# Rotary embedding on one core: the combines write bf16, and ScalarE widens the result to f32 before the store

## The chip, the cores and the metric

The kernel runs on one core of a Trainium2 chip. The metric is the device time of one execution in microseconds (us). The kernel before takes 165.52 us (median of 16 runs, 165.32 to 166.47). All runs named here are fast, with a granted clock of 1.0. The profiler's span is about 1.9 us shorter than the device time of the same run, so spans are compared with spans and times with times.

## The reference, cut to what matters

```python
# x: (16, 512, 1024) f32; cos, sin: (512, 32) f32; 16 heads of 64
x1, x2 = x[..., :32], x[..., 32:]          # per head
rotated = concatenate([x1 * cos - x2 * sin, x1 * sin + x2 * cos], axis=-1)   # f32
```

Each element is read once and written once: 33.55 MB in, 33.55 MB out, and 0.13 MB of tables. There is no matmul.

## The kernel before

One of the 16 batches is one tile: 128 partitions, four rows of 1024 f32 on each, 2 MB. SyncE's queue issues the loads, up to three tiles ahead. ScalarE (ACT) casts a tile to bf16 and issues the stores. VectorE (DVE) does four operations per tile: two multiplications (the products) and then a subtraction and an addition of their halves (here called the combines). The tables were widened once to 64 columns, each holding its 32 values twice.

```python
NX = 3    # buffers for loads       NC = 2   # casts
NO = 3    # results                 NTMP = 2 # products
# SyncE
for t in range(NT):
    if t >= NX: sp.wait_ge(sem_ci, t - NX + 1)          # cast t-3 done
    sp.dma_start(x_sb[:, xb, :], x_tile_ap(t)).then_inc(sem_in[xb], 16)
    # t == 0: also the two tables, 64 KB each
# ScalarE (the tables are cast first)
LEAD = 2
for it in range(NT + LEAD):
    t = it
    if t < NT:
        ae.wait_ge(sem_in[xb], 16 * (t // NX + 1))
        if t >= NC: ae.wait_ge(sem_vp, t - NC + 1)      # products t-2 done
        ae.activation(xb_sb[:, cb, :], x_sb[:, xb, :], ACT_COPY).then_inc(sem_ci, 1)
    u = it - LEAD
    if u >= 0:
        ae.wait_ge(sem_vf, u + 1)
        ae.dma_start(out_tile_ap(u), o_sb[:, ob, :]).then_inc(sem_out[ob], 16)
# VectorE (waits for buffers cut)
ve.tensor_tensor(t1v, xb_jhd(cb), coscat_b, mult)                           # L135
ve.tensor_tensor(t2v, xb_jhd(cb), sincat_b, mult).then_inc(sem_vp, 1)       # L136
ve.wait_ge(sem_vp, t + 1)
if t >= NO: ve.wait_ge(sem_out[ob], 16 * (t // NO))      # store t-3 landed
ve.tensor_tensor(orows[:, :, 0:HALF], t1[:, :, 0:HALF], t2[:, :, HALF:HD], subtract)       # L141
ve.tensor_tensor(orows[:, :, HALF:HD], t2[:, :, 0:HALF], t1[:, :, HALF:HD], add).then_inc(sem_vf, 1)  # L144
```

## Time and profile before

| | before |
|---|---|
| device time, median | 165.52 us |
| span of the profiled run | 164.6 us |
| VectorE busy | 142.5 us (87%) |
| ScalarE busy | 59.9 us (36%) |
| moved by DMA | 67.25 MB |

The page of the kernel before first gives the busy time of each engine; then the span in 40 slices, VectorE's busy tenths, DMA's busy tenths and the rate in GB/s.

```profile
DVE 142.5 (87%) x64; ACT 59.9 (36%) x21; POOL 0.2 (0%) x4
...
DVE  0007999999999999999999999999998989999930
...
DMA  5999999999999999999999999999999999999547
GB/s 171 434 418 422 442 438 366 422 430 434 438 430 418 446 426 438 418 438 430 442 422 426 442 430 430 422 436 434 434 422 430 438 438 426 418 446 382 255 191 318
```

Two rows of nines stand under each other: VectorE and DMA both look full. The groups of instructions of the kernel before: busy time in us and mean ns of one, then the idle time before them and what ended it.

```profile
L111 ACT ACTIVATE xb_sb<-x_sb 128x4096 bf16<-128x4096 f32 x16 | 57.8, 3615 | 74.2 <-DMA x_sb<-in_x_dram 37.6
L135 DVE TENSOR_TENSOR tmp_sb<-xb_sb,coscat_sb 128x4096 bf16<-128x4096 bf16 x16 | 36.6, 2285 | 13.2 <-ACT xb_sb L111 13.2
L141 DVE TENSOR_TENSOR o_sb<-tmp_sb 128x2048 f32<-128x2048 bf16 x16 | 36.7, 2292 | 2.2 <-DMA out_dram<-o_sb 1.6
L144 DVE TENSOR_TENSOR o_sb<-tmp_sb 128x2048 f32<-128x2048 bf16 x16 | 36.6, 2284 | 0.0
```

The combines have half the elements of the products and take the same time (2292 and 2284 ns for 2048 elements, 2285 ns for 4096). They differ in writing f32. The next view, the table of windows, shows whether DMA moves more where VectorE is not full. It gives length, busy time (and count) of VectorE, ScalarE and GpSimd, clock, DMA's busy share and GB/s of each stretch.

```profile
4.00:24.00 20.00, 10.78 (x5) 11.65 (x7) 0.00 (x0) 1.00 1.02 431
24.00:29.00 5.00, 4.96 (x4) 2.29 (x1) 0.00 (x0) 1.00 0.99 377
29.00:149.00 120.00, 117.89 (x54) 44.72 (x13) 0.00 (x0) 1.00 1.01 431
149.00:154.00 5.00, 4.97 (x3) 0.00 (x0) 0.00 (x0) 1.00 0.95 403
154.00:159.00 5.00, 3.86 (x2) 0.00 (x0) 0.00 (x0) 1.00 0.26 108
```

From 4 to 24 us VectorE is half idle, and DMA moves 431 GB/s. From 29 to 149 us VectorE is full, and DMA moves the same 431 GB/s. So 431 GB/s is what DMA gives in this kernel, whether VectorE is half idle or full. 67.25 MB at that rate is 156 us, to which the start comes (171 GB/s in the first of the 40 slices). That the rate is DMA's limit for these transfers rests on the two stretches here and on the run of the streams alone below, which has 432 GB/s from 29 to 149 us with no engine computing. After the start, the one large loss is at the end. Measured against 431 GB/s, the windows from 149 to 159 us lack (431-403)x5/431 + (431-108)x5/431 = 4.1 us of DMA's work. This missing work is called the hole below. The timeline of the kernel before says why (start, duration, engine, line):

```profile
155.58 2.29 DVE L144 TENSOR_TENSOR o_sb<-tmp_sb 128x2048 f32<-128x2048 bf16 x1
157.90 0.34 ACTq L116 DMA_DIRECT2D out_dram<-o_sb  x1
```

The loads end near 138 us. By the landing times in the trace, the stores of 4.5 tiles are left over then. The first 3.5 of them keep DMA busy until about 155 us, but VectorE releases the last one only at 157.9 us.

### The profile page before, as it was taken

What the parts mean: (1) busy time and instruction counts of PE and PEld (TensorE: products, weight loads), DVE (VectorE), ACT (ScalarE), POOL (GpSimd) and SP (SyncE); (2) the same over time, 40 slices, a digit from 0 to 9 for tenths busy, and PEclk for the clock granted to TensorE, in tenths of its full rate; (3) what the DMA queues carried; (4) which work ended last, traced back from release to release, by engine and by line L of the source; (5) the groups of instructions that cost most, each with busy time, mean ns of one, the idle gap of its engine ahead of it and who ended that gap; (6) DMA issues with size and microseconds to landing.
All of it is one profiled execution on the core that took longest, in us unless ns stands there. A gap on an engine that the chain in (4) does not pass through costs nothing.

```text
span 164.6 us, 190 instructions
## 1 busy us (share of the span) xinstructions
DVE 142.5 (87%) x64; ACT 59.9 (36%) x21; POOL 0.2 (0%) x4
## 2 busy tenths in 40 slices
DVE  0007999999999999999999999999998989999930
ACT  3088635335170808062433508052260804300000
POOL 0000000000000000000000000000000000000000
DMA  5999999999999999999999999999999999999547
GB/s 171 434 418 422 442 438 366 422 430 434 438 430 418 446 426 438 418 438 430 442 422 426 442 430 430 422 436 434 434 422 430 438 438 426 418 446 382 255 191 318
DMA packets 4897, 67.25 MB, mean 408 GB/s; under 512 B 544, under 2 KB 800, under 8 KB 800
## 3 DMA queue, kind: packets, MB, share of 16 engines
q1 hardware_dynamic: 2592, 33.69, 48.8%
q10 hardware_dynamic: 2304, 33.56, 47.7%
q14 instruction: 1, 0.01, 0.0%
HBM read 33.69 MB, written 33.55 MB: 408 GB/s over the span
## 4 chain that ended last, share of the span: by engine, by line
DMA 53%; DVE 25%; ACT 8%; issue 7%; DVEq 1%; SPq 0%; ACTq 0%
DMA x_sb<-in_x_dram 30%; DMA out_dram<-o_sb 19%; DVE tmp_sb L135 8%; DVE tmp_sb L136 8%; ACT xb_sb L111 8%; DVE o_sb L144 6%; DMA sin_sb<-in_sin_dram 4%; DVE o_sb L141 3%; DVEq L40 1%; SPq L88 0%; SPq L86 0%; ACT coscat_sb L96 0%; ACT sincat_sb L99 0%; ACT sincat_sb L98 0%; ACT coscat_sb L97 0%
## 5 line engine op out<-in xcount | busy, mean ns | idle before, releaser
L111 ACT ACTIVATE xb_sb<-x_sb 128x4096 bf16<-128x4096 f32 x16 | 57.8, 3615 | 74.2 <-DMA x_sb<-in_x_dram 37.6
L135 DVE TENSOR_TENSOR tmp_sb<-xb_sb,coscat_sb 128x4096 bf16<-128x4096 bf16 x16 | 36.6, 2285 | 13.2 <-ACT xb_sb L111 13.2
L141 DVE TENSOR_TENSOR o_sb<-tmp_sb 128x2048 f32<-128x2048 bf16 x16 | 36.7, 2292 | 2.2 <-DMA out_dram<-o_sb 1.6
L136 DVE TENSOR_TENSOR tmp_sb<-xb_sb,sincat_sb 128x4096 bf16<-128x4096 bf16 x16 | 36.6, 2285 | 0.0
L144 DVE TENSOR_TENSOR o_sb<-tmp_sb 128x2048 f32<-128x2048 bf16 x16 | 36.6, 2284 | 0.0
L96 ACT ACTIVATE coscat_sb<-cos_sb 128x128 bf16<-128x128 f32 x1 | 0.3, 309 | 6.6 <-DMA sin_sb<-in_sin_dram 6.6
L96 ACT ACT_TABLE_LOAD x1 | 1.3, 1283 | 0.7 <-PEq L162 0.7
L99 ACT ACTIVATE sincat_sb<-sin_sb 128x128 bf16<-128x128 f32 x1 | 0.3, 293 | 0.0
L97 ACT ACTIVATE coscat_sb<-cos_sb 128x128 bf16<-128x128 f32 x1 | 0.3, 292 | 0.0
L98 ACT ACTIVATE sincat_sb<-sin_sb 128x128 bf16<-128x128 f32 x1 | 0.3, 292 | 0.0
L162 POOL MEMSET const-bfloat16-1.0<- 128x1 bf16 x1 | 0.1, 102 | 0.0
L162 POOL MEMSET const-uint8-127<- 128x1 uint8 x1 | 0.1, 102 | 0.0
L162 POOL MEMSET const-float32-0.0<- 128x1 f32 x1 | 0.1, 99 | 0.2 <-issue 0.2
L162 POOL MEMSET const-float32-1.0<- 128x1 f32 x1 | 0.1, 99 | 0.0
## 6 DMA issues: line engine op xcount, KB each, us to landing
x_sb<-in_x_dram SPq DMA_DIRECT2D x16, 2048.0 KB, 21.2
out_dram<-o_sb ACTq DMA_DIRECT2D x16, 2048.0 KB, 17.8
cos_sb<-in_cos_dram SPq DMA_DIRECT2D x1, 64.0 KB, 7.3
sin_sb<-in_sin_dram SPq DMA_DIRECT2D x1, 64.0 KB, 7.0
```

Of the source, the lines that this page charges most:

```text
L40: with ExitStack() as stack:
L96: last = ae.activation(coscat_sb[:, :, 0:HALF], cos_sb[:, :, :], ACT_COPY)
L97: last = ae.activation(coscat_sb[:, :, HALF:HD], cos_sb[:, :, :], ACT_COPY)
L98: last = ae.activation(sincat_sb[:, :, 0:HALF], sin_sb[:, :, :], ACT_COPY)
L99: last = ae.activation(sincat_sb[:, :, HALF:HD], sin_sb[:, :, :], ACT_COPY)
L111: ae.activation(xb_sb[:, cb, :], x_sb[:, xb, :], ACT_COPY).then_inc(sem_ci, 1)
L135: ve.tensor_tensor(t1v, xb_jhd(cb), coscat_b, mult)
L136: ve.tensor_tensor(t2v, xb_jhd(cb), sincat_b, mult).then_inc(sem_vp, 1)
L141: ve.tensor_tensor(orows[:, :, 0:HALF], t1[:, :, 0:HALF], t2[:, :, HALF:HD], subtract)
L144: ve.tensor_tensor(orows[:, :, HALF:HD], t2[:, :, 0:HALF], t1[:, :, HALF:HD], add).then_inc(sem_vf, 1)
L162: nc = _bacc.Bacc("TRN2", target_bir_lowering=False, num_devices=1)
```

## The change

Its intent is to make VectorE's combines faster. They write a new bf16 tile `ob_sb`; ScalarE copies it to the f32 tile `o_sb` and issues the store. On ScalarE the copy out of tile t-2 now stands ahead of the cast of tile t. There are three cast buffers instead of two. A list of tiles is added that could split tiles, but all 16 stay whole. The core of the diff:

```diff
-    NC = 2
+    NC = 3
     NO = 3
+    NOB = 3
+        ob_sb = stack.enter_context(nc.sbuf_tensor([P, NOB, RE], bf16))
 ... (ScalarE's loop)
+                u = it - LEAD
+                if u >= 0:
+                    ae.wait_ge(sem_vf, u + 1)
+                    if u >= NO:
+                        ae.wait_ge(sem_out[ob], 16 * (u // NO))
+                    ae.activation(
+                        o_sb[:, ob, 0:Eu], ob_sb[:, obb, 0:Eu], ACT_COPY
+                    ).then_inc(sem_co, 1)
+                    ae.wait_ge(sem_co, u + 1)
+                    ae.dma_start(out_tile_ap(u), o_sb[:, ob, 0:Eu]).then_inc(sem_out[ob], 16)
                 t = it
                 if t < NT:
 ... (the cast, as before)
-                u = it - LEAD
-                if u >= 0:
-                    ae.wait_ge(sem_vf, u + 1)
-                    ae.dma_start(out_tile_ap(u), o_sb[:, ob, :]).then_inc(sem_out[ob], 16)
 ... (VectorE)
-                if t >= NO:
-                    ve.wait_ge(sem_out[ob], 16 * (t // NO))
+                if t >= NOB:
+                    ve.wait_ge(sem_co, t - NOB + 1)
+                obv = ob_sb[:, obb, 0:E].rearrange("p (r d) -> p r d", d=HD)
                 ve.tensor_tensor(
-                    orows[:, :, 0:HALF], t1[:, :, 0:HALF], t2[:, :, HALF:HD], subtract
+                    obv[:, :, 0:HALF], t1[:, :, 0:HALF], t2[:, :, HALF:HD], subtract
                 )
 ... (the addition likewise)
```

More of the change, by code (lines that the diff above doesn't have):

```diff
@@ L22, in bass_split_heads_rope_kernel, with _split @@
     SPP = seq // P
+    tiles = [(b, 0, SPP) for b in range(batch)]
+    def _split(tile, parts):
+        b, j0, nj = tile
+        if nj % parts != 0:
+            return [tile]
+        q = nj // parts
+        return [(b, j0 + i * q, q) for i in range(parts)]
+    if len(tiles) >= 2:
+        t_last = tiles.pop()
+        t_prev = tiles.pop()
+        tiles += [t_prev, t_last]
+    NT = len(tiles)
     ROWS = SPP * H
     RE = ROWS * HD
-    NT = batch
     NX = 3
-    NC = 2
+    NC = 3
     NO = 3
+    NOB = 3
     NTMP = 2
@@ L54, in bass_split_heads_rope_kernel @@
         sem_ci = stack.enter_context(nc.semaphore("sem_ci"))
+        sem_co = stack.enter_context(nc.semaphore("sem_co"))
         sem_vp = stack.enter_context(nc.semaphore("sem_vp"))
@@ L57, in bass_split_heads_rope_kernel @@
         block = stack.enter_context(nc.Block(no_gpsimd_drain=False))
-        cos_v = cos.rearrange("(p j) d -> p j d", p=P)
-        sin_v = sin.rearrange("(p j) d -> p j d", p=P)
+        cos_v = cos.rearrange("(p j) d -> p (j d)", p=P)
+        sin_v = sin.rearrange("(p j) d -> p (j d)", p=P)
         def x_tile_ap(t):
-            return x[t, :, :].rearrange("(p j) d -> p (j d)", p=P)
+            b, j0, nj = tiles[t]
+            v = x[b, :, :].rearrange("(p j) d -> p j d", p=P)
+            return v[:, j0:j0 + nj, :].rearrange("p j d -> p (j d)")
         def out_tile_ap(t):
-            return out[t, :, :, :].rearrange("(p j) h d -> p (j h d)", p=P)
-        def xb_jhd(cb):
-            return xb_sb[:, cb, :].rearrange("p (j h d) -> p j h d", j=SPP, h=H)
-        def o_rows(ob):
-            return o_sb[:, ob, :].rearrange("p (r d) -> p r d", d=HD)
-        coscat_b = coscat_sb[:, :, None, :].broadcast_to([P, SPP, H, HD])
-        sincat_b = sincat_sb[:, :, None, :].broadcast_to([P, SPP, H, HD])
+            b, j0, nj = tiles[t]
+            v = out[b, :, :, :].rearrange("(p j) h d -> p j (h d)", p=P)
+            return v[:, j0:j0 + nj, :].rearrange("p j e -> p (j e)")
         def uses(nbuf, b):
@@ L83, in _ @@
                 xb = t % NX
+                _, _, nj = tiles[t]
+                E = nj * H * HD
                 if t >= NX:
                     sp.wait_ge(sem_ci, t - NX + 1)
-                sp.dma_start(x_sb[:, xb, :], x_tile_ap(t)).then_inc(sem_in[xb], 16)
+                sp.dma_start(x_sb[:, xb, 0:E], x_tile_ap(t)).then_inc(sem_in[xb], 16)
                 if t == 0:
-                    sp.dma_start(cos_sb[:].rearrange("p j d -> p (j d)"),
-                                 cos_v.rearrange("p j d -> p (j d)")).then_inc(sem_tab, 16)
-                    sp.dma_start(sin_sb[:].rearrange("p j d -> p (j d)"),
-                                 sin_v.rearrange("p j d -> p (j d)")).then_inc(sem_tab, 16)
+                    sp.dma_start(
+                        cos_sb[:].rearrange("p j d -> p (j d)"), cos_v
+                    ).then_inc(sem_tab, 16)
+                    sp.dma_start(
+                        sin_sb[:].rearrange("p j d -> p (j d)"), sin_v
+                    ).then_inc(sem_tab, 16)
         @block.scalar
@@ L103, in _ @@
             for it in range(NT + LEAD):
+                u = it - LEAD
+                if u >= 0:
+                    ob = u % NO
+                    obb = u % NOB
+                    _, _, nju = tiles[u]
+                    Eu = nju * H * HD
+                    ae.wait_ge(sem_vf, u + 1)
[6 more added lines that the diff above has]
+                    ae.dma_start(out_tile_ap(u), o_sb[:, ob, 0:Eu]).then_inc(sem_out[ob], 16)
                 t = it
@@ L107, in _ @@
                     cb = t % NC
+                    _, _, nj = tiles[t]
+                    E = nj * H * HD
                     ae.wait_ge(sem_in[xb], 16 * (t // NX + 1))
@@ L110, in _ @@
                         ae.wait_ge(sem_vp, t - NC + 1)
-                    ae.activation(xb_sb[:, cb, :], x_sb[:, xb, :], ACT_COPY).then_inc(sem_ci, 1)
-                u = it - LEAD
-                if u >= 0:
-                    ob = u % NO
-                    ae.wait_ge(sem_vf, u + 1)
-                    ae.dma_start(out_tile_ap(u), o_sb[:, ob, :]).then_inc(sem_out[ob], 16)
+                    ae.activation(
+                        xb_sb[:, cb, 0:E], x_sb[:, xb, 0:E], ACT_COPY
+                    ).then_inc(sem_ci, 1)
             for b in range(NO):
@@ L122, in _ @@
             for t in range(NT):
+                bt, j0, nj = tiles[t]
+                R = nj * H
+                E = R * HD
                 cb = t % NC
                 tb = t % NTMP
-                ob = t % NO
+                obb = t % NOB
                 if t == 0:
@@ L130, in _ @@
                     ve.wait_ge(sem_vf, t - NTMP + 1)
-                t1 = tmp1_sb[:, tb, :, :]
-                t2 = tmp2_sb[:, tb, :, :]
-                t1v = t1.rearrange("p (j h) d -> p j h d", j=SPP)
-                t2v = t2.rearrange("p (j h) d -> p j h d", j=SPP)
-                ve.tensor_tensor(t1v, xb_jhd(cb), coscat_b, mult)
-                ve.tensor_tensor(t2v, xb_jhd(cb), sincat_b, mult).then_inc(sem_vp, 1)
+                xbv = xb_sb[:, cb, 0:E].rearrange("p (j h d) -> p j h d", j=nj, h=H)
+                t1 = tmp1_sb[:, tb, 0:R, :]
+                t2 = tmp2_sb[:, tb, 0:R, :]
+                t1v = t1.rearrange("p (j h) d -> p j h d", j=nj)
+                t2v = t2.rearrange("p (j h) d -> p j h d", j=nj)
+                cos_b = coscat_sb[:, j0:j0 + nj, None, :].broadcast_to([P, nj, H, HD])
+                sin_b = sincat_sb[:, j0:j0 + nj, None, :].broadcast_to([P, nj, H, HD])
+                ve.tensor_tensor(t1v, xbv, cos_b, mult)
+                ve.tensor_tensor(t2v, xbv, sin_b, mult).then_inc(sem_vp, 1)
                 ve.wait_ge(sem_vp, t + 1)
-                if t >= NO:
-                    ve.wait_ge(sem_out[ob], 16 * (t // NO))
-                orows = o_rows(ob)
+                if t >= NOB:
+                    ve.wait_ge(sem_co, t - NOB + 1)
+                obv = ob_sb[:, obb, 0:E].rearrange("p (r d) -> p r d", d=HD)
                 ve.tensor_tensor(
-                    orows[:, :, 0:HALF], t1[:, :, 0:HALF], t2[:, :, HALF:HD], subtract
+                    obv[:, :, 0:HALF], t1[:, :, 0:HALF], t2[:, :, HALF:HD], subtract
                 )
                 ve.tensor_tensor(
-                    orows[:, :, HALF:HD], t2[:, :, 0:HALF], t1[:, :, HALF:HD], add
+                    obv[:, :, HALF:HD], t2[:, :, 0:HALF], t1[:, :, HALF:HD], add
                 ).then_inc(sem_vf, 1)
```

## The prediction

> **What bounds it now.** VectorE looks like the limit (busy 142.5 of 164.6 us; its wait list shows almost nothing after the first 13.2 us), but DMA is at its limit at the same time. The table of windows has 431 GB/s from 4 to 24 us and again from 29 to 149 us; 67.25 MB at 431 GB/s is 156 us, so DMA alone needs about 158 to 160 us with its start. [...] ScalarE's casts wait for loads (37.6 us in total) as much as for VectorE (36.6 us). Only two stretches fall short of the rate: 24 to 29 us (377 GB/s, first store; loss 0.6 us) and the end. There the windows show 370 GB/s in 150-155 us and 39 GB/s in 155-158.8 us: all earlier stores are done while VectorE, 20 us behind the last load, finishes the last tile at 157.9 us; then one 2 MB store takes 6.3 us. The loss there is about 4 us. That gap is all a faster VectorE can win.
>
> **What the change does.**
> - L141/L144 (2292 and 2284 ns for 2048 elements, f32 output) now write bf16. L135/L136 do 4096 all-bf16 elements in 2285 ns, twice the rate, so I expect about 1.2 us each, 1.15 back to back. [...] VectorE per tile: 8.9 to about 6.8 us; busy 142.5 to about 108 us.
> - ScalarE gains 16 copies bf16 to f32 of 4096 elements; same size as the cast (3615 ns): busy 60 to about 118 us, 7.5 us per tile with issue and semaphore. Still under DMA's 9.75 us per tile (4.19 MB at 431 GB/s).
> - On ScalarE's queue the copy out of tile t-2 stands before the cast of tile t, and the copy out of t-1 waits behind the cast that waits for load t. Stores are delayed, but three loads or stores stay queued, so DMA does not starve. The third cast moves from 18.4 to about 24 us and load 5 from 22 to 27.7 us, just as load 4 ends: up to 0.7 us more loss where the first store ramps up.
> - NC 2 to 3 and the tile list change nothing by themselves (all tiles stay whole).
>
> **Critical path.** Middle: DMA, unchanged at 431 GB/s. Tail: last load lands near 137-138 us as before; cast 3.6, VectorE 6.8 (overlapping the copy out of tile 14), copy out 3.6: last store issued near 152 us instead of 157.9, before the store of tile 14 ends at about 155-156. The gap closes: -4 us. Start: +0 to +0.7 us. Net about -3.7 us.
>
> **Prediction: 161.9 us** (ratio 0.978), range 160.8 to 163.3. Faster by over 2%: 0.57; within 2%: 0.40; slower: 0.03. The 2% line (162.3) lies inside the uncertainty.
>
> **Signs.** Right: VectorE busy near 108 us, the two bf16 combines near 1.2 us; ScalarE near 118 us; middle windows still 431 GB/s; no window under 400 GB/s after 30 us until the last 2 us; the last store issued 150-153 us; chain of waits almost all DMA. VectorE now waits for ScalarE/loads.
>
> **What would make it wrong.** Combines stay at 2.3 us although bf16 (then the path after the last load grows by the copy: about 165-168 us). A start-up hole larger than 1 us, since DMA can't catch up. Stores delayed behind blocked casts so far that loads run dry, or the three store buffers block ScalarE: a hole in the middle. The last load landing later than 140 us leaves fewer stores to cover the last tile's 14 us: the gap would reopen.

The sum: -4 us at the end and 0 to +0.7 us at the start, about -3.7 us in all from 165.52 us, or 161.9 us. DMA's limit rests on the 431 GB/s of the two stretches. The combines' time of about 1.2 us is the author's estimate from the products: half of 2285 ns is 1.14 us, and the rest up to 1.2 us rests on no run before the result.

## The result, and the profile after

The changed kernel takes 162.47 us (median of 9 runs, 162.20 to 162.61). The ratio is 0.9804, with a 95% interval of 0.9787 to 0.9821: 2% lies inside the interval, so the verdict at 2% is "unclear", and the gain of 3 us itself is not in doubt. (A ratio is the mean time of one kernel's fast runs over that of the other's of the same rounds, so not quite the ratio of the medians quoted.)

The page of the changed kernel, the same parts:

```profile
DVE 109.6 (68%) x64; ACT 117.1 (73%) x37; POOL 0.2 (0%) x4
...
DVE  0006997989898989896929669294883939759100
...
DMA  5999999999999999999999999999999999999996
GB/s 147 411 451 441 421 437 400 429 425 433 429 437 425 433 433 425 441 425 433 433 425 437 429 433 431 425 437 429 433 433 423 437 429 433 433 421 441 429 433 270
```

VectorE's row of nines is gone, DMA's stays and now reaches to the last slice. The groups of the changed kernel:

```profile
L143 ACT ACTIVATE xb_sb<-x_sb 128x4096 bf16<-128x4096 f32 x16 | 57.9, 3616 | 15.5 <-DMA x_sb<-in_x_dram 12.7
L129 ACT ACTIVATE o_sb<-ob_sb 128x4096 f32<-128x4096 bf16 x16 | 57.8, 3610 | 12.6 <-DVE ob_sb L179 6.4
L176 DVE TENSOR_TENSOR ob_sb<-tmp_sb 128x2048 bf16<-128x2048 bf16 x16 | 19.6, 1225 | 0.6
L179 DVE TENSOR_TENSOR ob_sb<-tmp_sb 128x2048 bf16<-128x2048 bf16 x16 | 19.5, 1219 | 0.0
```

The first combine of a tile fell from 2292 to 1225 ns, the second, which follows it back to back, from 2284 to 1219 ns. ScalarE's busy time doubled, from 59.9 to 117.1 us. The table of windows of the changed kernel:

```profile
4.00:24.00 20.00, 10.54 (x6) 11.65 (x7) 0.00 (x0) 1.00 1.02 432
24.00:29.00 5.00, 4.01 (x4) 4.58 (x2) 0.00 (x0) 1.00 0.99 406
29.00:149.00 120.00, 94.90 (x56) 95.93 (x27) 0.00 (x0) 1.00 1.01 431
149.00:154.00 5.00, 0.13 (x1) 3.62 (x1) 0.00 (x0) 1.00 1.00 429
154.00:159.00 5.00, 0.00 (x0) 0.00 (x0) 0.00 (x0) 1.00 0.98 419
```

In the middle nothing changed: 431 GB/s, though VectorE does its work in 95 us instead of 118. From 149 to 159 us DMA lacks only 0.2 us of work. The timeline of the changed kernel at its end:

```profile
138.59 3.62 ACT L143 ACTIVATE xb_sb<-x_sb 128x4096 bf16<-128x4096 f32 x1 [1.56 <-DMA x_sb<-in_x_dram]
...
149.16 3.62 ACT L129 ACTIVATE o_sb<-ob_sb 128x4096 f32<-128x4096 bf16 x1 [3.45 <-DVE ob_sb L179]
152.81 0.34 ACTq L133 DMA_DIRECT2D out_dram<-o_sb  x1
```

The last load lands at 138.6 us, and the last store is issued at 152.8 us, 5 us earlier than before in spite of the added copy. By the landing times in the trace, the store of tile 14 ends at 155.2 us, so DMA goes over to the last store without a hole.

### The profile page after: what moved, and what is told of

The parts are those of the page before. It is cut to its first block, busy times and chain, and to the rows that moved or that the text cites. A ratio compares the mean times of both kernels' runs of the same rounds, so it can differ in the third digit from the quotient of the medians.

```text
span 160.4 us, 218 instructions
## 1 busy us (share of the span) xinstructions
DVE 109.6 (68%) x64; ACT 117.1 (73%) x37; POOL 0.2 (0%) x4
## 4 chain that ended last, share of the span: by engine, by line
DMA 50%; ACT 30%; DVE 7%; issue 6%; ACTq 1%; DVEq 1%; SPq 0%
DMA x_sb<-in_x_dram 45%; ACT xb_sb L143 16%; ACT o_sb L129 13%; DMA sin_sb<-in_sin_dram 5%; DVE tmp_sb L171 3%; DVE ob_sb L176 2%; DVE tmp_sb L170 1%; ACTq L133 1%; DVEq L55 1%; DVE ob_sb L179 1%; SPq L102 0%; SPq L100 0%; ACT coscat_sb L112 0%; ACT coscat_sb L113 0%; ACT sincat_sb L114 0%
## 5 line engine op out<-in xcount | busy, mean ns | idle before, releaser
L129 ACT ACTIVATE o_sb<-ob_sb 128x4096 f32<-128x4096 bf16 x16 | 57.8, 3610 | 12.6 <-DVE ob_sb L179 6.4
L170 DVE TENSOR_TENSOR tmp_sb<-xb_sb,coscat_sb 128x4096 bf16<-128x4096 bf16 x16 | 36.7, 2292 | 39.0 <-ACT xb_sb L143 39.0
L171 DVE TENSOR_TENSOR tmp_sb<-xb_sb,sincat_sb 128x4096 bf16<-128x4096 bf16 x16 | 36.5, 2284 | 0.0
L176 DVE TENSOR_TENSOR ob_sb<-tmp_sb 128x2048 bf16<-128x2048 bf16 x16 | 19.6, 1225 | 0.6
L179 DVE TENSOR_TENSOR ob_sb<-tmp_sb 128x2048 bf16<-128x2048 bf16 x16 | 19.5, 1219 | 0.0
```

Source lines behind the costliest of these rows:

```text
L129: ae.activation(o_sb[:, ob, 0:Eu], ob_sb[:, obb, 0:Eu], ACT_COPY).then_inc(sem_co, 1)
L170: ve.tensor_tensor(t1v, xbv, cos_b, mult)
L171: ve.tensor_tensor(t2v, xbv, sin_b, mult).then_inc(sem_vp, 1)
L176: ve.tensor_tensor(obv[:, :, 0:HALF], t1[:, :, 0:HALF], t2[:, :, HALF:HD], subtract)
L179: ve.tensor_tensor(obv[:, :, HALF:HD], t2[:, :, 0:HALF], t1[:, :, HALF:HD], add).then_inc(sem_vf, 1)
```

## The experiments

Theory A, that of the prediction: DMA at 431 GB/s is the limit of both kernels, and the change wins the hole at the end alone. Rival B: ScalarE's copies took back most of VectorE's gain, and DMA has room. Rival C: the gain comes from the faster VectorE, or from the third cast buffer, all along the run.

### The kernel before again

No edit.

> The kernel before, unchanged, for a second profile. The one on record was taken on a run of 166.47 us, the slowest of 16 (median 165.52). Theory A: a profile of a median run has a span of about 163.6 us and a hole in the stores near the end of about 3 us instead of 4. Ratio 1.00.

Measured: 165.54 us (ratio 0.9994); this profile is of a run of 165.32 us and has a span of 163.5 us. First its windows at the end, then all of VectorE's waits, from the list of waits (total us, times, longest), and its last combine.

```profile
149.00:154.00 5.00, 4.96 (x3) 0.00 (x0) 0.00 (x0) 1.00 0.99 426
154.00:159.00 5.00, 2.73 (x2) 0.00 (x0) 0.00 (x0) 1.00 0.39 164
...
DVE tmp_sb L135 <- ACT xb_sb L111: 13.5, 1, 13.5
DVE o_sb L141 <- DMA out_dram<-o_sb: 0.2, 1, 0.2
...
154.45 2.29 DVE L144 TENSOR_TENSOR o_sb<-tmp_sb 128x2048 f32<-128x2048 bf16 x1
```

The wait that differs is the one for earlier stores.
That wait was 1.6 us (the L141 group above).

The hole of an ordinary run is 0.06 + 3.10 = 3.2 us, not 4.1. In the run on record VectorE waited 1.6 us for earlier stores and so released the last one about 1.1 us later. The 16 runs fall in two groups (165.3 to 165.7 and 166.1 to 166.5), and the profile on record is of the slower one; the rounds of the experiments also have 165.90 and 165.97 us in between. What makes a run slow is open. The changed kernel's gain of 3.05 us is about the hole of an ordinary run, 3.2 us, less the 0.2 us that are left.

This profile also shows what theory A leaves out. VectorE starts its first product at 13.5 us, waits for 0.2 us after that, and ends at 156.7 us; from its issue to the end of the span are 6.8 us more, and 13.5 + 143.2 + 6.8 = 163.5 us is the whole span. So in the kernel before, VectorE's path is as long as the span: it sets the end, although DMA is full in the middle, and DMA's own work is only 3 us shorter (the changed kernel's span is 160.4 us). That theory A calls DMA the limit of both kernels is too strong for the kernel before. The change takes VectorE off the longest path, and what it wins is the distance to DMA's, which shows as the hole at the end.

### The streams alone

```diff
 # kernel before; ScalarE's and VectorE's work is taken out
-                    sp.wait_ge(sem_ci, t - NX + 1)
+                    sp.wait_ge(sem_in[xb], 16 * (t // NX))
 # ScalarE
+            ae.wait_ge(sem_vf, 1)                       # the memset
+            for u in range(NT):
+                ae.wait_ge(sem_in[u % NX], 16 * (u // NX + 1))
+                ae.dma_start(out_tile_ap(u), o_sb[:, ob, :]).then_inc(sem_out[ob], 16)
 # VectorE: one memset of o_sb
```

> Wrong result on purpose: all computing is taken out, the 16 loads, the two tables and the 16 stores of the same bytes stay; store t waits for load t alone. Theory A (DMA at its rate is the limit of both kernels): span 159.5 to 160.5 us, time about 161 to 162 us, within 1 us of the changed kernel. Theory B (ScalarE's added copies took the gain back; DMA has room): well under that, 150 us or less.

Measured: 162.64 us (4 runs, 162.38 to 163.27), span 160.6 us; the result is wrong. Its windows (no ScalarE column, as it does no counted work):

```profile
4.00:24.00 20.00, 9.66 (x1) 0.00 (x0) 1.00 1.01 416
...
29.00:149.00 120.00, 0.00 (x0) 0.00 (x0) 1.00 1.01 432
...
154.00:159.00 5.00, 0.00 (x0) 0.00 (x0) 1.00 0.99 423
```

The same transfers without any computing are no faster than the changed kernel. This run is not quite a lower bound: its stores wait for the memset, and its start lacks 20x(431-416)/431 = 0.7 us of DMA's work, where the changed kernel lacks 0.3 us (from 24 to 29 us). So faster engines could win some tenths of a microsecond at most while these bytes move in this way. Rival B falls.

### ScalarE's copy cut to an eighth

```diff
 # changed kernel; o_sb is zeroed once by GpSimd at the start
-                        o_sb[:, ob, 0:Eu], ob_sb[:, obb, 0:Eu], ACT_COPY
+                        o_sb[:, ob, 0:Eu // 8], ob_sb[:, obb, 0:Eu // 8], ACT_COPY
```

> Wrong result on purpose: the changed kernel with a copy out of 512 instead of 4096 elements (the store tiles are zeroed once at the start by GpSimd), so ScalarE has about 4.4 us per tile instead of 7.6. Theory A: within 1 us of the changed kernel, 161.5 to 162.5 us, as DMA is the limit. Theory B: clearly faster, 155 us or less.

Measured: 162.49 us, the changed kernel's time, with ScalarE busy 68.9 instead of 117.1 us (wrong result):

```profile
DVE 109.2 (68%) x64; ACT 68.9 (43%) x37; POOL 10.5 (7%) x5
```

With the whole copy, ScalarE's stores go out every 7.6 us at first (31.57 and 39.17 us in the changed kernel), which is under the 9.7 us that DMA needs per tile (4.19 MB at 431 GB/s). Its copies cost nothing here. Rival B falls a second time.

### Only the third cast buffer

```diff
 # kernel before
-    NC = 2
+    NC = 3
```

> The kernel before with three cast buffers instead of two, nothing else of the change. Theory A: no change (165.5 us, ratio 0.997 to 1.003), since VectorE, not the cast, is what the last store waits for. Theory C: a visible part of the 3 us.

Measured: 165.96 us, ratio 1.0026 (1.0008 to 1.0045): if anything slightly slower. The buffer wins nothing by itself, and that half of rival C falls.

### Only the end of the kernel before

```diff
 # kernel before; VectorE, last tile: the same four operations row by row
+                if t == NT - 1:
+                    for i in range(PIECES):          # 4 pieces, one row of each partition
+                        ve.tensor_tensor(t1v[:, i], xb_jhd(cb)[:, i], coscat_b[:, i], mult)
+                        ...                          # sin product, subtract, add
+                            .then_inc(sem_vf, 1)     # per piece
+                    continue
 # ScalarE, last tile
+                    for i in range(PIECES):
+                        ae.wait_ge(sem_vf, u + 1 + i)
+                        ae.dma_start(o_last[:, i, :], o_sb[:, ob, i * W:(i + 1) * W]).then_inc(sem_out[ob], 16)
```

> The kernel before, f32 combines and no copy out; only the last tile is combined and stored in four pieces, so that three quarters of its store run while VectorE still works. Theory A (only the hole in DMA's work at the end was won): span about 161 to 161.5 us, time about 162 to 163 us, most of the change's gain without its bf16 path; VectorE still busy about 143 us. Theory C (the gain comes from the faster VectorE or the third cast buffer all along the run): no gain beyond 1 us, about 165 us.

Measured: 163.20 us, ratio 0.985 (0.9824 to 0.9876), correct. Its page and windows:

```profile
DVE 143.6 (89%) x76; ACT 59.9 (37%) x21; POOL 0.2 (0%) x4
...
149.00:154.00 5.00, 4.93 (x9) 0.00 (x0) 0.00 (x0) 1.00 0.99 426
154.00:159.00 5.00, 4.06 (x7) 0.00 (x0) 0.00 (x0) 1.00 0.80 328
```

VectorE is as busy as ever, with f32 combines, and 2.4 of the 3.05 us are there. The missing part fits the 1.2 us of DMA's work that the window from 154 to 159 us still lacks. It is enough to give DMA something to store while VectorE works on the last tile. So neither faster combines all along the run nor the third buffer are needed for most of the gain, and rival C falls. The run does not tell apart the two ways to say what is won: it also shortens VectorE's path, as only a quarter of the last store follows its last combine (2.7 us from issue to landing, against 6.3 us before).

### The result tile shifted by one element

```diff
 # changed kernel
-        ob_sb = stack.enter_context(nc.sbuf_tensor([P, NOB, RE], bf16))
+        ob_sb = stack.enter_context(nc.sbuf_tensor([P, NOB, RE + 2], bf16))
-ob_sb[:, obb, 0:E]        # and 0:Eu on ScalarE
+ob_sb[:, obb, 1:1 + E]
```

> The changed kernel with the bf16 result tile shifted by one element (2 bytes); all else equal. If the combines lose their double rate for it, they take about 2.29 us each instead of 1.22, and theory A expects the hole at the end back and larger than before, since the copy out now comes on top: span about 167 to 168 us, time about 168 to 170 us, slower than the kernel before. If the combines stay at 1.22 us, the time stays at 162.5 us and the run says only that the alignment is not what the rate needs.

Measured: 162.45 us. This was meant to take the double rate away and leave the rest alone, and it didn't:

```profile
L176 DVE TENSOR_TENSOR ob_sb<-tmp_sb 128x2048 bf16<-128x2048 bf16 x16 | 20.4, 1273 | 0.6
L179 DVE TENSOR_TENSOR ob_sb<-tmp_sb 128x2048 bf16<-128x2048 bf16 x16 | 20.1, 1256 | 0.0
```

The combines lost 3 to 4% (1225 and 1219 ns before the shift), not half their rate. The run says nothing on theory A; the next one stands in for it.

### The copy without the faster combines

```diff
 # changed kernel
-        ob_sb = stack.enter_context(nc.sbuf_tensor([P, NOB, RE], bf16))
+        ob_sb = stack.enter_context(nc.sbuf_tensor([P, NOB, RE], fp32))
```

> The changed kernel with its intermediate tile in f32 instead of bf16: the copy out stays, the combines get f32 outputs again (expected 2.29 and 2.28 us instead of 1.22). It stands in for the shifted tile, which did not slow the combines. Theory A: the last tile's path after the last load grows by 2.1 us, and ScalarE, which waits for VectorE in turn, needs about 9 us per tile from the start: last store issued about 160 us, holes in DMA's work at 27-30 us and at the end, span about 167 to 168 us, time 168.5 to 170 us, slower than the kernel before. So the copy out alone costs, and only the bf16 combines pay for it.

Measured: 168.73 us, ratio 1.0185 (1.0163 to 1.0207). A combine group, the windows at the end, and the last issue from the timeline of this run:

```profile
L176 DVE TENSOR_TENSOR ob_sb<-tmp_sb 128x2048 f32<-128x2048 bf16 x16 | 36.7, 2292 | 0.6
...
149.00:154.00 5.00, 4.97 (x3) 2.20 (x1) 0.00 (x0) 1.00 0.89 377
154.00:159.00 5.00, 2.48 (x2) 2.48 (x1) 0.00 (x0) 1.00 0.56 239
...
160.16 0.34 ACTq L133 DMA_DIRECT2D out_dram<-o_sb  x1
```

Only the type between the engines differs from the changed kernel, and the time is 6.3 us up. The last store is issued at 160.2 us, 7.3 us later than in the changed kernel. VectorE sets the end again: from 13.5 us on it waits for nothing and ends at 156.5 us, then the copy takes 3.6 us and the last store 6.8 us, in all the span of 166.9 us. The copy out costs time on the path of the last tile, and the bf16 combines pay for it. One thing was expected wrongly: there is no hole at 27 to 30 us (the window from 24 to 29 us has 423 GB/s). DMA falls short from 32 to 52 us instead, and the window from 29 to 149 us has 423 GB/s, 2.2 us of work less.

### Two buffers for loads

```diff
 # changed kernel
-    NX = 3
+    NX = 2
```

> The changed kernel with two buffers for loads instead of three. Theory A: loads run ahead less, so fewer stores are left over when the last load lands (about 146 to 147 us instead of 138.6), too few to cover the last tile's 14 us: holes at the start (13 to 15 and near 25 us) and at the end, span about 167 to 168 us, time about 168 to 170 us, though no engine's work changes. A theory in which the busiest engine sets the time expects no change (162.5 us).

Measured: 170.26 us, ratio 1.0288. Four windows of this run, from the start to the end:

```profile
4.00:24.00 20.00, 10.43 (x6) 11.57 (x7) 0.00 (x0) 1.00 0.91 368
...
29.00:149.00 120.00, 88.29 (x52) 89.58 (x26) 0.00 (x0) 1.00 1.01 427
149.00:154.00 5.00, 2.80 (x2) 5.00 (x2) 0.00 (x0) 1.00 0.87 374
154.00:159.00 5.00, 4.06 (x3) 1.55 (x2) 0.00 (x0) 1.00 0.74 315
```

No engine has more work than in the changed kernel. The last cast, which waits for the last load, starts at 147.55 us instead of 138.59, so fewer stores are left to cover the 14 us that the last tile needs from landing to store. The hole at the end is back, with another one at the start. The changed kernel therefore needs its three load buffers: they let the loads run ahead and leave a stock of stores for the end. (The kernel before with two was not run.)

### Three attempts at a better version

They aim at the start, where the window from 24 to 29 us (the first store) has 406 GB/s.

First, in the changed kernel, the tables' loads moved from SyncE's queue to ScalarE's:

```diff
-                if t == 0: sp.dma_start(<cos>) ; sp.dma_start(<sin>)
+            ae.dma_start(<cos>) ; ae.dma_start(<sin>)      # ScalarE, before wait_ge(sem_tab, 32)
```

> The changed kernel with the two small table loads issued from ScalarE's queue instead of SyncE's, an attempt at a better version. If the slow ramp of the first store (first packet 3.6 us after issue, about 0.3 us of DMA's work lost at 26 to 28 us) comes from the first use of that queue, it goes: 0.2 to 0.5 us faster than the changed kernel (about 162.1 us). If not, the same 162.5 us.

Measured: 166.85 us, a clear miss. The DMA issues of this run (KB each, us to landing) and two windows:

```profile
sin_sb<-in_sin_dram ACTq DMA_DIRECT2D x1, 64.0 KB, 12.8
...
4.00:16.00 12.00, 0.00 (x0) 2.06 (x5) 0.00 (x0) 1.00 1.01 428
16.00:22.00 6.00, 3.54 (x2) 5.86 (x2) 0.00 (x0) 1.00 0.71 246
```

The table took 12.8 us to land instead of 7.3. Its queue moved only 9 to 16 GB/s from 3 to 13 us by the packet records, beside 16 KB rows on the other queue: 251 of its packets of 512 bytes started in that time, and 250 rows. 256 such packets over 16 DMA engines are 16 for each; if each waits for one row packet (median 0.611 us in the changed kernel's packet records), that is an estimated 9.8 us, which fits. The first cast then starts at 14.75 us, three loads fill all buffers, and DMA runs dry from 16 to 22 us. By the windows, 6x(431-246)/431 = 2.6 us are lost there, and nothing makes them up; the middle of this run is also slower (424 GB/s from 29 to 149 us, worth 1.9 us), for a cause that was not followed up.

Second, the first tile's load in two halves of 64 partitions, one on each queue:

```diff
+                if t == 0: sp.dma_start(x_sb[0:P // 2, xb, 0:E], x_tile_ap(t)[0:P // 2]).then_inc(sem_in[xb], 16)
+            ae.dma_start(x_sb[P // 2:P, 0, :], x_tile_ap(0)[P // 2:P]).then_inc(sem_in0b, 16)
 ... (ScalarE waits for sem_in0b before the first cast)
```

> The changed kernel with the first tile's load issued as two halves of 64 partitions, one from SyncE's queue and one from ScalarE's, an attempt at a better version: both queues have been used once when the first store comes, and no 512-byte packet waits beside full rows for long. If the slow start of a queue's first transfer is what costs 0.3 to 0.5 us at 26-28 us, and perhaps part of the first load's slow start, 0.2 to 0.8 us faster than the changed kernel (161.7 to 162.3 us). If the slow start belongs to the transfer direction or the memory, no change. If the tables land later than 9 us, as in the run before, slower.

Measured: 166.93 us. The window from 4 to 24 us of this run:

```profile
4.00:24.00 20.00, 5.87 (x4) 8.03 (x6) 0.00 (x0) 1.00 1.02 334
```

DMA's busy share is full at a lower rate, and 20x(431-334)/431 = 4.5 us are lost, which is the whole difference. By the packet records, the halves went one after the other, from 2.1 to 7.1 us and from 6.7 to 12.1 us, which is 207 and 192 GB/s; most 16 KB packets took 1.1 to 1.3 us instead of 0.61. Why halves of 64 partitions move in this way is not shown; the next run, with halves of all 128 partitions on the same two queues, has 432 GB/s from 4 to 24 us.

Third, the same halves by columns, all 128 partitions each:

```diff
+                if t == 0: sp.dma_start(x_sb[:, xb, 0:E // 2], x_tile_ap(t)[:, 0:E // 2]).then_inc(sem_in[xb], 16)
+            ae.dma_start(x_sb[:, 0, RE // 2:RE], x_tile_ap(0)[:, RE // 2:RE]).then_inc(sem_in0b, 16)
 ... (the wait as before)
```

> The changed kernel with the first tile's load in two halves by columns (all 128 partitions each), one from SyncE's queue, one from ScalarE's: the run before without its halves by partitions[...]. If a queue's first use is what makes the first store ramp up slowly (406 GB/s at 24-29 us in the changed kernel against 431), the window 24-29 us is at 425 or more and the time 0.2 to 0.5 us below the changed kernel (about 162.0 to 162.3 us). If the slow ramp belongs to storing as such, the window stays near 406 and the time at 162.5 us or, if the tables come later than 9 us, above.

Measured: 162.38 us (162.18 to 162.70), the changed kernel's time. One window:

```profile
24.00:29.00 5.00, 4.04 (x4) 4.58 (x3) 0.00 (x0) 1.00 1.00 423
```

The window from 24 to 29 us rose from 406 to 423 GB/s, which is worth 5x(423-406)/431 = 0.2 us, but the time doesn't show it. Its tables came 0.4 us later, and its span in the profile is 160.9 us. A queue's first use is not the main cause of the slow first store: by the packet records, the first store's first packet starts 2.9 us after its issue here and 3.5 us after it in the run before, against 3.6 us in the changed kernel (24.0 to 27.6 us; its first load's first packet starts 1.0 us after issue, 0.7 to 1.7 us), although ScalarE's queue had been used in both. In the run with the tables on that queue it was 0.9 us, and there the load before the store was nearly through. What sets it stays open. No version beat the changed kernel beyond the noise, as the run of the streams alone made likely.

## Why the prediction was right, and where it was off

The measured 162.47 us lies inside the range of 160.8 to 163.3, and 0.6 us above the central 161.9.

- **DMA is at its limit at the same time as VectorE, and a faster VectorE can win only the gap at the end.** Right: 431 GB/s in the middle of both kernels, and the streams alone take 162.64 us. What the prediction does not say is that VectorE's path of 143 us, from 13.5 us on, is as long as the span and sets the end of the kernel before.
- **Combines near 1.2 us, VectorE busy near 108 us.** Right: 1.225 and 1.219 us, 109.6 us.
- **ScalarE busy near 118 us and not the limit.** Right: 117.1 us, and an eighth of the copy gives 162.49 us.
- **Last load near 137 to 138 us, last store issued near 152 us, no hole.** Right: 138.6 and 152.8 us.
- **"The gap closes: -4 us."** The gap closed but for 0.2 us, and its size was off. It was read from a profile whose run, with 166.47 us, was the slowest, and taken off the median of all runs. An ordinary run's hole is 3.2 us, so 3.0 us were won here where 4 were forecast. This probably is also why a gain over 2% was called the likelier outcome (0.57) and the measurement fell on the line.
- **"Start: +0 to +0.7 us."** It was about 0: the window from 24 to 29 us has 406 GB/s in the changed kernel, 406 in the second profile of the kernel before, 377 in the first. The forecast sum had about 0.3 us of loss here, which hid a third of the error in the gap: that the centre was missed by only 0.6 us is in part luck.
- **"Chain of waits almost all DMA."** Wrong. The chain of the kernel before, then of the changed kernel:

```profile
DMA 53%; DVE 25%; ACT 8%; issue 7%; DVEq 1%; SPq 0%; ACTq 0%
```

```profile
DMA 50%; ACT 30%; DVE 7%; issue 6%; ACTq 1%; DVEq 1%; SPq 0%
```

The chain runs through ScalarE for 30% of the span, and yet cutting ScalarE's busy time by 48 us moved nothing. So this chain did not say what a faster ScalarE would win. The kernel before shows how little one chain fixes: its second profile has DMA at 42% and VectorE at 33%.
- **Combines that stay slow "about 165-168 us".** The run with f32 in between had slow combines and took 168.73 us: the direction was right, and the size was a little above what was said. VectorE's path from 13.5 us, with the copy of 3.6 us behind it, accounts for it.

## What to carry to other kernels

When two resources are both busy all along, divide the bytes by the rate that DMA reaches while the other resource is half idle, and add what DMA loses at the start and the end even with no engine in its way (156 us and some 4 us here, by the changed kernel's span of 160.4 us). What remains between that and the span is what a faster engine can win: here 163.5 - 160.4 = 3.1 us of an ordinary run, in the last 10 us. Then add up the other resource's own path, from its first work to the last store: in the kernel before it was as long as the span. Check it with a kernel that moves the same bytes and computes nothing, and see whether a change to the last tile alone wins as much. Before you take microseconds off a median, look which run the profile belongs to: here it was the slowest of 16, which was worth 1 us of the 3.
